# A float32 decoder trunk: two kinds of elementwise work moved from VectorE to adding transfers

## The chip, the cores and the metric

The kernel runs on one core of one Trainium2 chip. The metric is device microseconds of one execution. Three executions of the kernel before took 2245.96, 2246.11 and 2246.87 us; their median, 2246.11 us, is the time before.

## The reference

The program computes two layers of a decoder trunk in float32, over 528 tokens (16 learned meta tokens and 512 others) of 1024 features. Each layer has a feed-forward, a gated pair of mixers (a short convolution and an attention) and a second feed-forward, each with a layer norm behind it:

```python
def swiglu(x, w_up, w_down):
    gate, up = jnp.split(x @ w_up, 2, axis=-1)
    return (jax.nn.silu(gate) * up) @ w_down

for l in range(DEPTH):                       # DEPTH = 2, ALPHA = (2 * DEPTH) ** 0.25
    h = layer_norm(ALPHA * h + 0.5 * swiglu(h, ffn1_w_up[l], ffn1_w_down[l]), ln_g[l, 0], ln_b[l, 0])
    ...
    h = layer_norm(ALPHA * h + mix, ln_g[l, 1], ln_b[l, 1])
    h = layer_norm(ALPHA * h + 0.5 * swiglu(h, ffn2_w_up[l], ffn2_w_down[l]), ln_g[l, 2], ln_b[l, 2])
```

`w_up` is 1024 x 5632 (2816 gate and 2816 up features), `w_down` is 2816 x 1024. The change lies in the four feed-forwards only.

## The kernel before

Activations lie with their features on the partitions. A float32 product is run as three passes of float32r: each operand is split into hi (rounded to 12 significant bits) and lo (the exact rest), and hi\*hi, hi\*lo and lo\*hi are summed in PSUM (`mm3`, L90 to L93). A weight tile of 512 KB is loaded by SyncE into a float32 tile `raw` (`load`, L105), ScalarE casts it to `wh` (L111) and VectorE subtracts to get `wl` (L114); `operand` does both.

Four `raw` tiles (pool `rawp`) and four pairs of `wh`, `wl` (pool `wp`) serve the up products. The down weights use a pool of their own, `dp`, with two pairs and two raw tiles; two of the raw tiles of the up products come from that pool too, those for u2 and for the sum S1.

A feed-forward treats its 2816 features as 11 pairs of tiles. The first two pairs go through `up_start`; the other nine through `up_seven`, which makes gate and up of a pair by seven products of half the contraction (Winograd's form). It loads four tiles g1, u2, u1, g2 and forms four sums of them on VectorE: S1 = u1 + u2 (L431), S3 = g1 - u1 (L432, over u1), S2 = S1 - g1 (L433, over g1), S4 = g2 - S2 (L441, over g2). S1 is the operand of the sixth product in the order M1, M6, gate A, M7, up A, M5, M3. The other factors are splits of sums of the activations that Pool forms (L337) and ScalarE and VectorE split (L88).

The down products of a chunk of pairs run between the up products of the next chunk: `mid[0]` behind M6 and `mid[1]` behind M5, each with its weights split by `operand(weights(...), dp)` in `steps`. Their results are added to the residual `r` (L558 with the scaling in the first chunk, L564 later). In the first chunk the first feature tile also gives a shift for the norm: `shift_by` casts that tile to bfloat16 on VectorE (L253), one product spreads its mean (L254), ScalarE copies it (L256) and Pool subtracts it from `r` (L561). This happens once for each of the two token ranges. In the last feed-forward the down products have the tokens on the partitions and no shift.

A scheduler orders the instructions of each engine before the run, from the program's order and its own estimates of when each one is ready; on the chip each engine then runs its own list in that order. SyncE issues all weight loads; Pool issues a few small transfers and none in the feed-forwards but two near the end.

Of the kernel before, what the change touches and what calls it, by code (L numbers as in the profile page):

```python
# [14 lines left out]
AF = mybir.ActivationFunctionType  # L15
ALU = mybir.AluOpType
AX = mybir.AxisListType

P = 128
# [18 lines left out]
# token ranges (first, width): all tokens, and those behind the meta tokens  # L38
FULL = ((0, 256), (256, 272))
TRIM = ((16, 256), (272, 256))  # L40
# and in two equal parts
EVEN = {FULL: ((0, 264), (264, 264)), TRIM: TRIM}
# chunks of the feed-forward features, in pairs of tiles
# [8 lines left out]
def trunk(ctx: ExitStack, tc: tile.TileContext, x, meta, f1_up, f1_dn, w_in, b_gate, conv_w, qn_g, w_uq,  # L52
          kvn_g, w_ukv, w_bc, w_bm, w_o, f2_up, f2_dn, ln_g, ln_b, rope, out):
    """Float32 products run as three passes of float32r: an operand is hi + lo, hi its value rounded to 12
    significant bits and lo the exact rest, and hi*hi + hi*lo + lo*hi are summed in PSUM. Activations lie with
    their features on the partitions."""
# [8 lines left out]
    @contextmanager  # L65
    def scratch(n, t):
        """The eight banks of PSUM, n for psum() and the others for psum2(), and t tiles in SBUF."""
        with tc.tile_pool(name="psp", bufs=1, space=bass.MemoryType.PSUM, reuse_waits="tile") as pool, \
                tc.tile_pool(name="tmp", bufs=t, reuse_waits="tile") as tp:
            banks.append((pool, n))  # L70
            tps.append(tp)
            yield
            banks.pop()
            tps.pop()
# [23 lines left out]
    def unit(pool=wp, k=8, c=P):  # L98
        """A stationary operand, hi and lo, as [128, k, c]."""
        return [pool.tile([P, 1024], F32R, name=n)[:, :k * c].rearrange("p (k c) -> p k c", c=c)  # L100
                for n in ("wh", "wl")]
# [6 lines left out]
    def operand(raw, pool=wp, cut=1):  # L108
        """Split, in parts where others would wait for long."""
        u = unit(pool, raw.shape[1], raw.shape[2])  # L110
        S.copy(u[0], raw)  # L111
        n = raw.shape[1] // cut
        for k in range(0, raw.shape[1], n):
            V.tensor_tensor(u[1][:, k:k + n], raw[:, k:k + n], u[0][:, k:k + n].bitcast(F32), op=ALU.subtract)  # L114
        return u

    def columns(src, c, pool=wp):
        """128 columns of a matrix with 1024 rows."""
        return operand(load(src[:, c:c + P], KD, P), pool)

# [10 lines left out]
    # per-feature parameters as columns  # L131
# [11 lines left out]
    def tokens_in(xt, c0):  # L143
        """Two tiles of tokens, to the columns from c0."""
# [14 lines left out]
    with tc.tile_pool(name="xload", bufs=1, reuse_waits="tile") as xp, scratch(4, 1):  # L159
# [8 lines left out]
        # the array's clock falls while it waits for the first products' operands: of no use but for that  # L168
# [3 lines left out]
    def rest_in(pool):  # L172
        """The other tokens, and the parameters."""
# [21 lines left out]
    # Per-token statistics are taken with the tokens on the partitions, n of them in each of nt columns, and  # L195
    # spread back over the partitions of the features.
# [5 lines left out]
    def token_sums(ps, at, parts, n, nt):  # L202
        """Columns at, at + 2, ...: the means over D features of the parts together."""
# [6 lines left out]
    def spread(c, n, nt, act, ps):  # L210
        """c / D on all partitions."""
# [10 lines left out]
    def rsqrt(v, n, nt, by=float(D)):  # L222
        """by/sqrt(v): the exponent trick, a Newton step, and a step of third order."""
# [13 lines left out]
    class Norm:  # L237
        """Layer norm over the features of r, which holds twice the sum to norm. The sums of r and of its squares
        are taken as its last parts come; by then r has been moved by a value near the mean of each token, which
        keeps the variance exact."""  # L240
# [7 lines left out]
        def shift_by(self, q0, w, i):  # L248
            """The mean of the first features of each token, on all partitions: near the mean, so that a rounded
            one does."""  # L250
# [22 lines left out]
        def run(self, q0, w):  # L273
            """The rest, in steps between which the tensor engine should have something else to do."""
# [44 lines left out]
    def project_steps(ps, u, nk, rhs, q0, w, n=4):  # L319
        """The same, with a stop after each n of the products' parts."""  # L320
# [7 lines left out]
    def combos(hv, th, tl):  # L328
        """Sums and differences of the parts of x (halves of its features, 1 and 2, and of its tokens, A and B)
        that the seven products take, split, from r that holds x. By index: T1 = x1B - x1A,  # L330
        T2 = x2B - T1, T3 = x2B - x1B, -T4 = x2A - T2."""
# [8 lines left out]
    def up_start(hp, dp, w_up, hv, pending, th, tl, after, begin):  # L340
        """silu(gate) * up for the first two pairs of feature tiles. What the first tokens allow comes first."""
# [62 lines left out]
    def up_seven(hp, fp, w_up, f, hv, mid, th, tl):  # L404
        """silu(gate) * up for two feature tiles by seven products of halves (Winograd's form): rows are gate and
        up, the contraction is halved, columns are the two token ranges."""
# [20 lines left out]
        product(pa, operand(g1), x1a, True)              # M1  # L427
        for j in range(2):
            S.copy(m1[j], pa[j])
        s1 = raw_tile(fp).rearrange("p (k c) -> p k c", c=256)  # L430
        V.tensor_tensor(s1, u1, u2, op=ALU.add)          # S1  # L431
        V.tensor_tensor(u1, g1, u1, op=ALU.subtract)     # S3  # L432
        V.tensor_tensor(g1, s1, g1, op=ALU.subtract)     # S2  # L433
        product(pb, operand(g1), t2, True)               # M6
# [5 lines left out]
        product(pa, operand(g2), x2a, False)             # gate A  # L440
        V.tensor_tensor(g2, g2, g1, op=ALU.subtract)     # S4  # L441
        for j in range(2):
            S.activation(sg[j], pa[j], AF.Silu)
        product(pb, operand(u1), t3, False)              # M7
        for j in range(2):
            V.tensor_tensor(u3s[j], pb[j], m1[j], op=ALU.add)
        product(pb, operand(u2), nt4, False)             # up A but for M1
        for j in range(2):
            hh, hl = hs[j]
            V.tensor_tensor(m1[j], pb[j], m1[j], op=ALU.add)     # up A  # L450
            V.tensor_tensor(sg[j], sg[j], m1[j], op=ALU.mult)
            split(hh[:, qa:qa + w], hl[:, qa:qa + w], sg[j])
# [3 lines left out]
        product(pc, operand(s1), t1, True)               # M5  # L456
        if mid[2]:
            mid[3]()
        for j in range(2):
            V.tensor_tensor(u3s[j], pc[j], u3s[j], op=ALU.add)   # up B  # L460
        if not mid[2]:
            mid[1]()
        product(pc, operand(g2, wp, 2), x2b, False)             # M5 + M3
        if mid[2]:
            mid[3]()
        for j in range(2):
            hh, hl = hs[j]
            V.tensor_tensor(u2s[j], pc[j], u2s[j], op=ALU.add)   # gate B
# [5 lines left out]
    def ffn(l, w_up, w_dn, idx, hv, pending, tail=None):  # L474
        """r = 2 alpha x + swiglu(x), and its norm. The down products of a chunk run between the up products of the
        next. With tail, the last step: tokens go back to the partitions."""
        with tc.tile_pool(name="ffn_t", bufs=1, reuse_waits="tile") as ttp, \
# [17 lines left out]
            def steps(ci, hs, mps, parts=(0, 1)):  # L495
                def step(_=None):
                    for mp in mps:
                        u = by_tile(operand(weights(ci, mp, rawp), dp), len(hs))
# [84 lines left out]
    def down_tokens(l):  # L583
        """The last step's down products, with tokens on the partitions, and its norm."""
        rt = r.rearrange("p k t -> p (k t)")[:, 0:4 * D].rearrange("p (i d) -> p i d", d=D)

        def make(dp):
# [18 lines left out]
            def begin():  # L606
                """The residual, token tile by token tile, where the features' x was."""
# [28 lines left out]
            def end(tiles):  # L636
                """The norm of some tiles up to the scaling by the deviation, which is returned."""
# [36 lines left out]
    def gate(l, hv, wi, i, m2, dst, ps_of):  # L674
        """tanh of half the gates' arguments of two feature tiles: sigmoid(z) = (tanh(z / 2) + 1) / 2."""
# [7 lines left out]
    def attention(l, hv, wi, ap, yc, ym, pending):  # L683
# [39 lines left out]
        def filler():  # L723
            """The rest of the convolution's branch and the first gate, a few products at a time."""
# [46 lines left out]
        # strip[p, c]: masked where p > c - 128; strip2[p, c]: masked where c - 384 > p  # L771
# [9 lines left out]
        # keys and queries of a head: rows 0..63 plain, 64..95 rotary, 96 the maximum against -1  # L781
# [7 lines left out]
        with tc.tile_pool(name="low", bufs=1, reuse_waits="tile") as lp, \  # L789
# [6 lines left out]
            def first(part):  # L796
                """The projections, and the sums of squares of those that are normed."""
# [70 lines left out]
    def heads_in(l, hv, wi, ap, ckn, cqn, kt, zt, ym, filler, cosT, sinT,  # L868
                 strip, strip2):
        # keys and queries of 16 tokens, of two heads, whole: from row 97 on the unit matrix and the mask  # L870
# [11 lines left out]
        def group_weights(g):  # L882
            """Of four heads: keys and values and plain queries in one unit, rotary queries and their swap."""
# [17 lines left out]
        def values(ua):  # L901
            """Values by key tile, split, each with ones beside it; of the tokens that end a part whole as well."""
# [19 lines left out]
        def rotary(ub):  # L922
            """Rotary parts of the queries of four heads, 32 rows each."""
# [34 lines left out]
        def maxima(b):  # L958
            """The largest score of each query, into a column of zt."""
# [19 lines left out]
        def maxima_rows():  # L979
            """The maxima into row 96 of the queries."""  # L980
# [11 lines left out]
        def units(b, q0, w):  # L992
            """The key tiles of a head that 64 queries or more of a part see."""
            return [(b, k0) for k0 in KTILES[:4] if k0 < q0 + w - 64]

        def end_of(q0, w):
            """The last 16 queries of a part, where they see 16 keys of one tile more, their own: which."""
# [3 lines left out]
        def score(q0, w, b, k0):  # L1001
            """Exponentials of the masked scores of a key tile, split."""
# [14 lines left out]
        def score_end(s0):  # L1017
            """Exponentials of the scores of 16 tokens among themselves, of both heads."""
# [11 lines left out]
        def normal(pr, q0, w, a, b):  # L1030
            """Both heads of a pair: divide by the sums."""
# [16 lines left out]
        def weigh(job, vals, pr):  # L1048
            """Products with the values, and at the end of a part of the queries its division."""
# [124 lines left out]
def _rope_rows():  # L1174
    """Rotary factors by position, for four heads of 32 rows: the cosines and the signed sines."""
# [23 lines left out]
```

## Time and profile before

| | |
|---|---|
| median of the runs | 2246.11 us |
| span of the profiled execution | 2247.7 us |
| TensorE matmul busy | 2202.0 us (98%), 17989 instructions |
| VectorE busy | 1679.5 us (75%) |
| ScalarE busy | 974.5 us (43%) |
| Pool busy | 372.6 us (17%) |
| transfers | 202.80 MB, mean 90 GB/s; SyncE's queue 28.2% of 16 engines |

The profiled execution is one more execution than the three timed ones; of it the page gives the span, which is 1.6 us over the median. Busy time is the time in which an engine had an instruction of its own running; waits, semaphores and the issue of transfers do not count. Matmuls overlap each other, so a row's duration is longer than the distance to the next one. Names such as L114 are lines of the kernel before.

### The profile page before, as it was taken

Reading aid. Unit: us, or ns where it says so; the run is one execution under the profiler, and the core shown is the slowest. Engines: PE = TensorE matmul, PEld = TensorE weight load, DVE = VectorE, ACT = ScalarE, POOL = GpSimd, SP = SyncE. Lnnn points to the kernel's source line nnn. Section 1 sums busy time; section 2 is a strip of 40 time slices with the busy share of each in tenths; the row PEclk is TensorE's granted clock in tenths of the full one; section 3 lists DMA queues with packets and bytes.
Section 4 is the critical chain, followed back from the end, with each engine's and each line's share of the span. In section 5 each row is a group of like instructions: output and inputs, shape, how many; then the busy total and the mean of one; then the engine's idle time right before and its main releaser. Section 6 shows DMA issues by size and latency. Waiting matters only on the chain. (4 is left out here: it accounts for less than half of the span.)

```text
span 2247.7 us, 43950 instructions
## 1 busy us (share of the span) xinstructions
PE 2202.0 (98%) x17989; PEld 2181.9 (97%) x17989; DVE 1679.5 (75%) x3191; ACT 974.5 (43%) x1881; POOL 372.6 (17%) x487
## 2 busy tenths in 40 slices
PE   9999999999999999999999999999999999999998
PEld 8999999999999999999999999999999999999998
DVE  6777778876646777878778778787665568877887
ACT  4343344465533543434353433444655335443441
POOL 3210004211014512000242100042110155100000
PEclk9999999999999999999999999999999999999999
DMA  5232232222233223323323232322222332233322
GB/s 172 94 103 91 90 119 77 68 62 67 69 92 104 66 82 98 113 75 111 107 66 95 96 98 90 113 85 63 66 67 76 94 94 85 76 103 105 99 90 86
DMA packets 237418, 202.80 MB, mean 90 GB/s; under 512 B 6990, under 2 KB 233360, under 8 KB 237216
## 3 DMA queue, kind: packets, MB, share of 16 engines
q1 hardware_dynamic: 234880, 195.65, 28.2%
q0 software_dynamic: 2336, 4.34, 0.7%
q8 instruction: 141, 2.31, 0.4%
q14 instruction: 61, 0.50, 0.1%
HBM read 195.74 MB, written 2.10 MB: 88 GB/s over the span
## 5 line engine op out<-in xcount | busy, mean ns | idle before, releaser
L114 DVE TENSOR_TENSOR wl<-raw,wh 128x1024 fp32r<-128x1024 f32 (+1 forms) x490 | 560.5, 1145 | 250.0 <-ACT wh L111 248.5
L111 ACT CAST wh<-raw 128x1024 fp32r<-128x1024 f32 (+1 forms) x454 | 466.2, 1034 | 591.2 <-PE ps L92 174.3
L92 PE MATMUL ps<-xl,wh 128*128 128x256 f32 (+2 forms) x1760 | 501.7, 285 | 2.7 <-DVE xl L88 2.7
L91 PE MATMUL ps<-xh,wh 128*128 128x256 f32 (+2 forms) x1760 | 502.5, 286 | 0.1
L93 PE MATMUL ps<-xh,wl 128*128 128x256 f32 (+2 forms) x1760 | 501.6, 285 | 0.0
L92 PEld LDWEIGHTS ps<-xl,wh 128*128 128x128 f32 x1760 | 332.5, 189 | 4.3 <-DVE xl L88 4.0
L91 PEld LDWEIGHTS ps<-xh,wh 128*128 128x128 f32 x1760 | 333.0, 189 | 0.6 <-ACT xh L88 0.5
L93 PEld LDWEIGHTS ps<-xh,wl 128*128 128x128 f32 x1760 | 333.4, 189 | 0.0
L91 PE MATMUL ps<-th,wh 128*128 128x264 f32 (+1 forms) x1152 | 328.5, 285 | 0.0
L92 PE MATMUL ps<-tl,wh 128*128 128x264 f32 (+1 forms) x1152 | 327.6, 284 | 0.0
L93 PE MATMUL ps<-th,wl 128*128 128x264 f32 (+1 forms) x1152 | 326.9, 284 | 0.0
L91 PE MATMUL pf<-hh,wh 128*128 128x256 f32 (+1 forms) x864 | 246.7, 286 | 0.0
L93 PE MATMUL pf<-hh,wl 128*128 128x256 f32 (+1 forms) x864 | 246.3, 285 | 0.0
L92 PE MATMUL pf<-hl,wh 128*128 128x256 f32 (+1 forms) x864 | 245.3, 284 | 0.0
L92 PEld LDWEIGHTS ps<-tl,wh 128*128 128x128 f32 x1152 | 218.8, 190 | 0.0
L91 PEld LDWEIGHTS ps<-th,wh 128*128 128x128 f32 x1152 | 218.6, 190 | 0.1
L93 PEld LDWEIGHTS ps<-th,wl 128*128 128x128 f32 x1152 | 218.3, 189 | 0.0
L91 PE MATMUL pf<-xh,wh 128*128 128x256 f32 (+1 forms) x640 | 188.0, 294 | 0.0
L92 PE MATMUL pf<-xl,wh 128*128 128x256 f32 (+1 forms) x640 | 184.4, 288 | 0.0
L93 PE MATMUL pf<-xh,wl 128*128 128x256 f32 (+1 forms) x640 | 183.2, 286 | 0.0
L91 PEld LDWEIGHTS pf<-hh,wh 128*128 128x128 f32 x864 | 162.7, 188 | 0.0
L93 PEld LDWEIGHTS pf<-hh,wl 128*128 128x128 f32 x864 | 162.7, 188 | 0.0
(323 smaller groups left out, 4870.3 us busy)
## 6 DMA issues: line engine op xcount, KB each, us to landing
raw<-in_ffn_w_up_dram SPq DMA_DIRECT2D x176, 512.0 KB, 3.6
raw<-in_ffn_w_down_dram SPq DMA_DIRECT2D x80, 512.0 KB, 3.3
raw<-in_mix_w_in_dram SPq DMA_DIRECT2D x64, 512.0 KB, 3.7
raw<-in_w_o_dram SPq DMA_DIRECT2D x16, 512.0 KB, 3.9
raw<-in_ffn_w_down_dram SPq DMA_DIRECT2D x16, 256.0 KB, 2.6
raw<-in_w_br_conv_dram SPq DMA_DIRECT2D x8, 512.0 KB, 3.3
raw<-in_w_br_mla_dram SPq DMA_DIRECT2D x8, 512.0 KB, 3.3
out_dram<-r SPq DMA_DIRECT2D x8, 256.0 KB, 2.4
```

Source lines behind the costliest of these rows:

```text
L91: PE.matmul(ps, lhsT=lhs[0], rhs=rhs[0], start=first, stop=False, skip_group_check=more)
L92: PE.matmul(ps, lhsT=lhs[0], rhs=rhs[1], start=False, stop=False, skip_group_check=more)
L93: PE.matmul(ps, lhsT=lhs[1], rhs=rhs[0], start=False, stop=last, skip_group_check=more)
L111: S.copy(u[0], raw)
L114: V.tensor_tensor(u[1][:, k:k + n], raw[:, k:k + n], u[0][:, k:k + n].bitcast(F32), op=ALU.subtract)
```

## The change

Two edits, beside comments that are taken out. The down weights of all chunks but the last (80 operands) go through a new function: ScalarE writes -hi into `wl`, a transfer issued by Pool adds the raw tile to it, and ScalarE writes hi into `wh`. S1 is no longer a VectorE addition of u1 and u2: u1's part of the matrix is loaded a second time, into the tile of S1, and a transfer issued by Pool adds u2 to it. This happens 36 times.

```diff
+    def operand_dma(raw, pool=wp):
+        u = unit(pool, raw.shape[1], raw.shape[2])
+        S.activation(u[1], raw, AF.Copy, scale=-1.0)
+        G.dma_start(u[1], raw, accum_op=ALU.add)
+        S.copy(u[0], raw)
+        return u
...
-        s1 = raw_tile(fp).rearrange("p (k c) -> p k c", c=256)
-        V.tensor_tensor(s1, u1, u2, op=ALU.add)          # S1
-        V.tensor_tensor(u1, g1, u1, op=ALU.subtract)     # S3
+        s1 = load(w_up[0:512, D_FF + f * P:D_FF + f * P + 256], KH, 256, fp)
+        G.dma_start(s1, u2, accum_op=ALU.add)
+        V.tensor_tensor(u1, g1, u1, op=ALU.subtract)
...
-                        u = by_tile(operand(weights(ci, mp, rawp), dp), len(hs))
+                        u = by_tile(operand_dma(weights(ci, mp, rawp), dp), len(hs))
```

## Rows read from the trace of the kernel before

**Rows 1.** Busy time by engine in one steady pair (instructions), clock, DMA share, GB/s.
```profile
128.60:160.70 32.10, 32.10 (x267) 32.10 (x266) 25.87 (x41) 12.43 (x20) 3.54 (x3) 1.00 0.32 99
```

**Rows 2.** What TensorE waited for: us in total, times, longest us.
```profile
PE pf L219 <- DVE t L218: 11.1, 13, 1.9
PE ps L254 <- DVE t L253: 7.3, 3, 2.7
...
PE ps L92 <- DVE xl L88: 2.7, 6, 0.7
```

**Rows 3.** VectorE in order of time around the first such wait: start, duration, line.
```profile
72.53 0.29 DVE L253 CAST t<-r 128x256 bf16<-128x256 f32 x1
75.67 1.23 DVE L431 TENSOR_TENSOR raw<-raw 128x1024 f32<-128x1024 f32 x1 [2.84 <-DMA raw<-in_ffn_w_up_dram]
...
77.14 1.22 DVE L432 TENSOR_TENSOR raw<-raw 128x1024 f32<-128x1024 f32 x1
78.28 0.78 DVE L558 SCALAR_TENSOR_TENSOR r<-r,pf 128x272 f32<-128x272 f32 x2
78.97 0.82 DVE L253 CAST t<-r 128x272 bf16<-128x272 f32 x1
```

**Rows 4.** The stretches behind the three waits: columns as in rows 1.
```profile
80.00:82.00 2.00, 2.00 (x10) 2.00 (x10) 0.00 (x0) 1.39 (x3) 1.25 (x2) 0.50 0.00 0
830.00:832.00 2.00, 2.00 (x12) 2.00 (x12) 0.20 (x1) 1.66 (x3) 1.37 (x2) 0.54 0.00 0
1205.00:1207.00 2.00, 2.00 (x14) 2.00 (x14) 0.62 (x1) 1.62 (x3) 1.50 (x2) 0.66 0.01 4
```

**Rows 5.** VectorE groups by shape: count, busy us, mean ns, idle before.
```profile
L114 DVE TENSOR_TENSOR wl<-raw,wh 128x1024 fp32r<-128x1024 f32 x402 | 499.5, 1244 | 196.8 <-ACT wh L111 196.1
L114 DVE TENSOR_TENSOR wl<-raw,wh 128x512 fp32r<-128x512 f32 x88 | 61.0, 693 | 53.2 <-ACT wh L111 52.4
...
L431 DVE TENSOR_TENSOR raw<-raw 128x1024 f32<-128x1024 f32 x36 | 45.5, 1264 | 39.2 <-DMA raw<-in_ffn_w_up_dram 37.4 <-issue 1.5 <-DVE r L599 0.3
```

**Rows 6.** SyncE's issues of the four up loads ahead of rows 3.
```profile
62.59 0.37 SPq L105 DMA_DIRECT2D raw<-in_ffn_w_up_dram  x1
67.76 1.89 SPq L105 DMA_DIRECT2D raw<-in_ffn_w_up_dram  x2
70.38 0.37 SPq L105 DMA_DIRECT2D raw<-in_ffn_w_up_dram  x1
```

**Rows 7.** Transfers by line: count, KB each, median us from issue to landing.
```profile
raw<-in_ffn_w_up_dram SPq DMA_DIRECT2D x176, 512.0 KB, 3.6
...
qt<-qrl POOLq DMA_DIRECT2D x8, 64.0 KB, 2.3
...
wl<-in_ln_b_dram POOLq DMA_DIRECT2D x1, 512.0 KB, 5.2
```

**Rows 8.** ScalarE in order of time: a steady pair's cast of down weights.
```profile
152.15 1.05 ACT L111 CAST wh<-raw 128x1024 fp32r<-128x1024 f32 x1 [2.08 <-DMA raw<-in_ffn_w_down_dram]
```

**Rows 9.** TensorE in order of time: first down product, first of M3.
```profile
169.33 0.28 PE L91 MATMUL pf<-hh,wh 128*128 128x256 f32 x1
...
192.71 0.28 PE L91 MATMUL ps<-xh,wh 128*128 128x264 f32 x1
```

**Rows 10.** VectorE in order of time, in the same steady pair.
```profile
170.55 1.22 DVE L114 TENSOR_TENSOR wl<-raw,wh 128x1024 fp32r<-128x1024 f32 x1 [0.52 <-ACT wh L111]
...
183.72 1.22 DVE L433 TENSOR_TENSOR raw<-raw 128x1024 f32<-128x1024 f32 x1
...
187.40 0.77 DVE L460 TENSOR_TENSOR t<-ps,t 128x264 f32<-128x264 f32 x2
```

**Rows 11.** VectorE in order of time, in the first pair of the first feed-forward.
```profile
45.98 1.22 DVE L433 TENSOR_TENSOR raw<-raw 128x1024 f32<-128x1024 f32 x1
...
48.39 1.23 DVE L114 TENSOR_TENSOR wl<-raw,wh 128x1024 fp32r<-128x1024 f32 x1 [0.84 <-ACT wh L111]
50.54 1.23 DVE L114 TENSOR_TENSOR wl<-raw,wh 128x1024 fp32r<-128x1024 f32 x1 [0.92 <-ACT wh L111]
```

## The prediction

> **What bounds the kernel now.** I looked first at the busy time in one steady stretch, then at what TensorE waited for, then at the costliest VectorE groups, and last at the order of time around each TensorE wait. One pair of feature tiles in the feed-forward takes 32.10 us, and TensorE is busy for all of it with 267 matmuls, 0.120 us each [rows 1]. VectorE is busy 25.87 us of it, ScalarE 12.43, Pool 3.54, the DMA engines 0.32. So work taken off VectorE inside a steady pair buys nothing by itself: what can be won is only the time in which TensorE stands. The waits of TensorE name it [rows 2]: 11.1 us in the norms, 7.3 us in three waits for the cast at L253, 2.7 us for parts of x. Only the last two stand beside an instruction that the change removes.
>
> **The three waits.** They fall once in each of the first three feed-forwards, where the first down products give the shift of the norm. In order of time VectorE casts the first shift operand at 72.53, then sits idle 2.84 us until a load of up weights has landed, does S1 (L431) at 75.67, then three residual updates (L558) with S3 (L432, 77.14) between them, and the second cast at 78.97 [rows 3]. TensorE needs that second cast and stands. The granted clock says that the stop costs more than its length: behind the three waits it is 0.50, 0.54 and 0.66 over two microseconds, so the lower level of 1.2 GHz for most of the stretch, after TensorE had idled over 2 us; in these stretches it did 10, 12 and 14 matmuls [rows 4] where 2.00 / 0.120 = 16.7 fit. That is (6.7 + 4.7 + 2.7) x 0.120 = 1.7 us more. The three places hold 7.3 + 1.7 = 9.0 us.
>
> **The change part by part.**
> *S1 leaves VectorE.* 36 additions go, 45.5 us in all, with 39.2 us of idle time before them [rows 5]. Which load did S1 wait for? It reads u1 and u2. u1, g1 and g2 share the four raw tiles, u2 takes the pool of the down weights. The four loads go out at 62.59, 67.76, 69.28 (the row's 67.76 + 1.89 - 0.37) and 70.38 [rows 6]; a load lands after 3.6 us [rows 7]. I read the last one as u2's, which has to wait for its own pool: landing near 74, and near 75.6 with three loads in flight. S3 = g1 - u1 does not need u2. It takes S1's place behind the first cast with u1 landed at the latest by 69.28 + 3.6 = 72.9. Then S3 runs 72.9 to 74.1 (1.22), the three updates take 1.2 as now (0.78 for two), and the second cast is done at about 75.7 instead of 79.8. TensorE's wait of 2.7 us ended with that cast (78.97 + 0.82 = 79.8), so it began at 77.1: the wait goes with 1.4 us to spare, and with it the slow stretch: -9.0 us over three places. What is late next there: nothing that I find; the operands of the following products stand ready well ahead (17 us for the one looked at below).
>
> *The lo parts of the down weights leave VectorE.* 80 operands (64 of 1024 columns, 16 of 512) times 1244 and 693 ns [rows 5] are 79.6 + 11.1 = 90.7 us. All lie beside TensorE work, so 0 us, and the loss of it is no gain. ScalarE takes a second pass of 1.05 us in its place [rows 8], 64 x 1.05 + 16 x about half of it = 76 us, raising its 12.43 us of 32.10 by 2.1: room enough, 0 us.
>
> *The adding transfer.* The trace shows none. As the lower bound I take the 64 KB transfer between tiles on Pool's queue, 2.3 us; as the upper one twice the slower 512 KB transfer on that queue, 2 x 5.2 = 10.4 us, since it reads both operands [rows 7]. I take 5.2, the row nearest in size and queue.
> The Trainium skill's page "Collectives: The Full Stack" (The bandwidth ceiling: the fold count and why AG ≠ RS ≠ AR) says that an add in the DMA path runs at half the copy rate because it needs two source reads; by that the transfer lies near the upper end, and the sum would be the 2240 to 2241 worked out below for it. No run here shows an add.
> For the down weights: the hi of the next pair's first unit is cast at 152.15 [rows 8] and its product starts at 169.33 [rows 9], 17.2 us later. Two ScalarE passes and 10.4 us from issue to landing need 12.5. So lo is in time even at the upper end: 0 us. The raw tile is held longer, by the transfer less the old subtraction, 5.2 - 1.2 = 4 us (9 at the upper end). The load at 62.59 goes into such a tile; it moves to about 66.6, still ahead of the one at 67.76, and at the upper end it passes that one by 4 us, which the 1.4 us to spare do not cover: u1 would land at 71.8 + 3.6 = 75.4, the second cast end at 78.1, and 1 us of each wait stay, 2240 to 2241 in all.
> For S1: its load takes the slot that is free after the subtraction at 170.55 [rows 10], so 171.8 + 3.6 = 175.4, and the adding transfer lands at 180.6. S2 (L433), which now waits for it, stands at 183.72 because it overwrites g1, so it has 3.1 us of margin at 5.2 us and is 2.1 us late at 10.4. Queued behind S2 on VectorE are the evacuations, first of all L460 at 187.40, which TensorE needs before M3 at 192.71 [rows 9, 10]: 5 us more. So a steady pair loses nothing up to some 13 us: 0 us.
> In the first pair of a feed-forward S2 stands at 45.98 and VectorE has gaps of only 0.84 and 0.92 us ahead of the passes at 48.39 and 50.54 [rows 11]; both loads are possible long before, as their pool is empty there, so 0 us, with a price below.
>
> *Traffic and Pool.* A pair moves six tiles of 512 KB now at a DMA share of 0.32; one load and three transfers more make 10/6 of it, 0.53, or 0.69 if an add counts twice. Not full: 0 us. Pool issues 116 transfers more, three or four to a pair in which it is busy 3.54 us. In the first down chunk the transfers share its queue with the residual updates that wait for the shift; those write r, which no product of that chunk reads, so a delay there costs 0 us.
>
> *Sum.* The span is 2247.7 us, 1.6 above the median of 2246.11 that I forecast from; the difference is carried over as it is. 2246.1 - 9.0 = **2237.1 us**.
>
> **The rivals.**
> *No gain (2246).* S1's place in the order was chosen by the scheduler from its own estimates; with S1 gone it may put something else there, a lo pass or S3 behind later loads (the retained raw tiles speak for it), and the second cast comes as late as now. For it: the 1.4 us to spare are few. Against it: the named wait is for one particular load. A part of the gain would read 2241 to 2246.
> *Slower at the first pairs (2253).* If the load or the transfer of S1 is put behind other work in its queue at the start of a feed-forward, S2 waits, and the splits of the token combinations, queued behind it, come late for the second product. It decides where the lateness exceeds the two gaps, 0.84 + 0.92 = 1.8 us. At the upper end of the transfer, 5.2 us later than taken, it is 5.2 - 1.8 = 3.4 us at each of four places, and a slow stretch of 0.6 us each: +16, less 9 if the other gain still comes, 2253.
> *Slower in every pair (2300).* The same transfer above 13 us, because it also changes the number format. At 15 us each of the 32 steady pairs loses 2 us: 2237 + 64 = 2301. For it: nothing here shows an add or a change of format. Against it: the 512 KB transfers of [rows 7] land in 3.6 and 5.2 us.
> *The transfer doesn't give lo* (it may round raw before the add): that would spoil digits but cost the same time.
>
> **How the numbers follow.** Chances: forecast 0.50, no gain 0.27, slower at first pairs 0.14, slower everywhere 0.09. The forecast's own range is 2233 (the 2.7 us at parts of x go as well, where S1 also stands in line, and a slow stretch behind them) to 2242. The range 2233 to 2254 leaves out the case in every pair and the worse half of the one at the first pairs. A difference of 0.2%, 4.5 us, is what a measurement can tell: below 2241.6 lies most of the forecast, 0.47; between, the no-gain case with its edges, 0.32; above 2250.6 the rest, 0.21.
>
> **What would show it.** Right: no wait for the cast at L253 in TensorE's list and a granted clock near 1.00 where it was 0.50; L432 close behind the first cast with no long wait for a load; VectorE's busy time lower by about 136 us and ScalarE's higher by 76, with TensorE's busy time unchanged. The transfers should land in about 5 us, and L433 should wait for them in no steady pair. Wrong: L253 still named, with another line in S1's place; new TensorE waits at the second product of the first pair; or L433 idle on a transfer in pair after pair.

## The result, and the profile after

The changed kernel takes 2319.12 us (median of four, 2314.39 to 2323.78), the kernel before 2246.49 in the same comparison: 1.0324 times as long, 95% interval 1.0308 to 1.0341. That is 72.6 us slower, where 9 us faster was forecast, and beyond every case that was priced, the worst of which was 2301. Lines of the kernel after are those of before plus 8 from L117 of before on: S1's transfer is L439, S3 L440, S2 L441, S4 L449, the evacuation behind M7 (VectorE's reading of that product out of PSUM) L454; -hi of a down weight is L120, its transfer L121, a token sum L345.

The head of the page of the kernel after:

```profile
span 2315.2 us, 44380 instructions
...
PE 2214.6 (96%) x17989; PEld 2190.3 (95%) x17989; DVE 1567.3 (68%) x3075; ACT 1041.0 (45%) x1961; POOL 456.9 (20%) x603
```

TensorE does the same 17989 matmuls, and Pool's 603 instructions are the 487 of before and the 116 issues. Of the 67.5 us by which the span grew, its busy time holds 12.6 (2214.6 - 2202.0) and its idle time 54.9 (100.6 - 45.7). VectorE has 112 us less to do, and the kernel is slower: the time is in waits.

What TensorE waits for after (columns as in [rows 2]):

```profile
PE ps L91 <- DVE t L454: 40.5, 13, 8.6
PE ps L91 <- DVE t L379: 14.4, 3, 4.8
PE pf L625 <- DVE t L623: 7.6, 1, 7.6
```

The norms' row is about that of before (10.3 us for 11.1). The three waits for the cast are gone. L454 and L379 are new, and the one at L625 was 3.4. With two smaller new rows, 5.6 together, that is 40.5 + 14.4 + 4.2 + 5.6 = 64.7 us more; the casts' 7.3 and the 2.7 at xl of [rows 2] went: 54.7, close to the 54.9 us of added idle time. A steady pair of after, and two stretches behind new waits (columns as in [rows 1]):

```profile
128.60:160.70 32.10, 32.10 (x264) 31.90 (x263) 21.35 (x37) 14.49 (x23) 7.41 (x7) 1.00 0.66 165
68.00:70.00 2.00, 2.00 (x11) 2.00 (x10) 1.54 (x3) 1.92 (x3) 0.00 (x0) 0.50 1.03 205
231.00:233.00 2.00, 1.84 (x8) 1.84 (x9) 2.00 (x4) 0.00 (x0) 0.00 (x0) 0.50 0.04 8
```

A steady pair is as full as in [rows 1], with VectorE 4.5 us less busy. Behind a wait the granted clock is 0.50, the level of 1.2 GHz, and 11 or 8 matmuls stand where 18 or 19 stand at 1.00 (before, 84 to 90 us): the busy time that grew. VectorE of after around the first shift, in order of time:

```profile
77.24 1.22 DVE L440 TENSOR_TENSOR raw<-raw 128x1024 f32<-128x1024 f32 x1 [2.30 <-DMA raw<-in_ffn_w_up_dram]
...
80.30 0.29 DVE L261 CAST t<-r 128x256 bf16<-128x256 f32 x1
...
81.31 0.30 DVE L261 CAST t<-r 128x272 bf16<-128x272 f32 x1
```

Transfers of after by line (count, KB each, median us to landing):

```profile
raw<-in_ffn_w_up_dram SPq DMA_DIRECT2D x212, 512.0 KB, 4.4
...
wl<-raw POOLq DMA_DIRECT2D x64, 512.0 KB, 4.8
...
raw<-raw POOLq DMA_DIRECT2D x36, 512.0 KB, 4.8
...
wl<-raw POOLq DMA_DIRECT2D x16, 256.0 KB, 3.2
```

Both casts now stand behind S3, 1.0 us apart, where [rows 3] had S1 and S3 between them. The wait is gone, as forecast, but here not by the forecast's way: S3 stands ahead of the first cast and has waited for a load, the second cast ends at 81.6 and not at 75.7, and TensorE, late itself by then, takes it at 84.3. The forecast's times show in e2 below. The price of a transfer came true, 4.8 us for the 5.2 taken.

**Place A: the start of a feed-forward.** Pool in order of time (start, duration, line, and in brackets the idle time before with what ended it), after:

```profile
38.35 0.93 POOL L439 DMA_DIRECT2D raw<-raw  x1 [33.04 <-PE ps L93]
38.96 1.10 POOL L345 TENSOR_TENSOR t<-r 128x264 f32<-128x264 f32 x1
51.05 0.89 POOL L121 DMA_DIRECT2D wl<-raw  x1 [10.99 <-ACT t L373]
51.67 1.06 POOL L345 TENSOR_TENSOR t<-r,t 128x264 f32<-128x264 f32 x1
...
63.83 0.93 POOL L345 TENSOR_TENSOR t<-r,t 128x264 f32<-128x264 f32 x1
```

The same of before:

```profile
22.58 0.76 POOL L337 TENSOR_TENSOR t<-r 128x264 f32<-128x264 f32 x1 [17.31 <-DVE r L191]
31.29 0.75 POOL L337 TENSOR_TENSOR t<-r,t 128x264 f32<-128x264 f32 x1 [7.95 <-DVE r L191]
...
56.77 0.95 POOL L337 TENSOR_TENSOR t<-r,t 128x264 f32<-128x264 f32 x1
```

After, the first sum stands behind S1's transfer and the second behind a down weight's transfer, which waits for ScalarE's -hi. ScalarE of after, -hi:

```profile
49.70 1.05 ACT L120 ACTIVATE wl<-raw 128x1024 fp32r<-128x1024 f32 x1
```

All sums but the first, spread from 31 to 58 before, are done from 51.67 to 64.8. Their splits on VectorE end at 66.4, and behind them in its list stands L379 (the product of gate and up), for which TensorE waits until 66.81, the first of the two rows below. This comes three times, 4.8 us each; in the last feed-forward the wait of 7.6 us at L625 takes its place.

**Place B: a chunk of one pair.** TensorE of after at the two places, in order of time:

```profile
66.81 0.59 PE L91 MATMUL ps<-xh,wh 128*128 128x264 f32 x1 [4.82 <-DVE t L379]
...
231.16 0.59 PE L91 MATMUL ps<-th,wh 128*128 128x264 f32 x1 [5.91 <-DVE t L454]
```

SyncE's loads ahead of the second place:

```profile
211.34 0.37 SPq L105 DMA_DIRECT2D raw<-in_ffn_w_up_dram  x1
224.36 0.37 SPq L105 DMA_DIRECT2D raw<-in_ffn_w_up_dram  x1
```

VectorE there:

```profile
228.94 1.22 DVE L440 TENSOR_TENSOR raw<-raw 128x1024 f32<-128x1024 f32 x1 [9.02 <-DMA raw<-in_ffn_w_up_dram]
...
230.68 0.43 DVE L454 TENSOR_TENSOR t<-ps,t 128x264 f32<-128x264 f32 x1
```

VectorE has nothing to do for 9.02 us, because S3 of the *next* pair is next in its list and its load was issued at 224.36, after SyncE had waited for a raw tile. Behind it, with one lo part between, stands the evacuation of *this* pair's M7, which needs nothing that comes late but TensorE's result, and TensorE cannot go on without it. This comes in the chunk of one pair of all four feed-forwards: these four of the 13 waits at L454, 5.2 to 8.6 us, make 25.4 of the 40.5. The next longest, 4.6 us at 1520.59, ends a feed-forward's last pair, where no S3 follows; its evacuation stands behind splits of the last down weights.

The kernel before has S3 ahead of the evacuations too:

```profile
215.89 1.22 DVE L432 TENSOR_TENSOR raw<-raw 128x1024 f32<-128x1024 f32 x1
...
217.89 0.42 DVE L446 TENSOR_TENSOR t<-ps,t 128x264 f32<-128x264 f32 x1
```

There the load had landed, and the order cost nothing. At the place above a tile is held for longer than a transfer's own time: on Pool the down weight's transfer of 217.94 stood behind S1's of 217.39, ahead of which Pool had idled 11.4 us. SyncE's waits for a held raw tile over the run of the kernel after (us in total, times, longest):

```profile
SPq L105 <- DMA wl<-raw: 578.9, 78, 17.1
```

VectorE's, at S3 and S2:

```profile
DVE raw L440 <- DMA raw<-in_ffn_w_up_dram: 94.0, 30, 11.6
...
DVE raw L441 <- DMA raw<-raw: 57.6, 17, 5.3
```

### The profile page after: what moved, and what is told of

Its sections match the earlier page's. It is cut to its first block, busy times and chain, and to the rows that moved or that the text cites. A ratio compares the mean times of both kernels' runs of the same rounds, so it can differ in the third digit from the quotient of the medians.

```text
span 2315.2 us, 44380 instructions
## 1 busy us (share of the span) xinstructions
PE 2214.6 (96%) x17989; PEld 2190.3 (95%) x17989; DVE 1567.3 (68%) x3075; ACT 1041.0 (45%) x1961; POOL 456.9 (20%) x603
## 3 DMA queue, kind: packets, MB, share of 16 engines
q1 hardware_dynamic: 253888, 214.53, 30.5%
q0 software_dynamic: 19040, 60.97, 13.6%
## 4 chain that ended last, share of the span: by engine, by line
PE 62%; DVE 9%; DMA 8%; issue 2%; ACT 2%; POOL 0%; DVEq 0%; POOLq 0%; ACTq 0%; SPq 0%
PE ps L91 13%; PE ps L92 13%; PE ps L93 13%; PE pf L91 6%; PE pf L92 6%; PE pf L93 6%; DMA raw<-in_ffn_w_up_dram 3%; DMA raw<-raw 2%; DVE wl L114 2%; DVE tl L88 2%; DMA wl<-raw 2%; DMA raw<-in_ffn_w_down_dram 1%; ACT wh L111 1%; PE ps L978 1%; PE ps L1014 1%
## 5 line engine op out<-in xcount | busy, mean ns | idle before, releaser
L114 DVE TENSOR_TENSOR wl<-raw,wh 128x1024 fp32r<-128x1024 f32 (+1 forms) x410 | 476.4, 1163 | 242.6 <-ACT wh L111 241.1
L111 ACT CAST wh<-raw 128x1024 fp32r<-128x1024 f32 x374 | 390.4, 1047 | 363.6 <-PE ps L92 163.3
L91 PE MATMUL ps<-xh,wh 128*128 128x256 f32 (+2 forms) x1760 | 506.2, 288 | 19.0 <-DVE t L379 14.4
L91 PE MATMUL ps<-th,wh 128*128 128x264 f32 (+1 forms) x1152 | 333.3, 289 | 41.8 <-DVE t L454 40.5
L121 POOL DMA_DIRECT2D wl<-raw x80 | 70.5, 881 | 575.0 <-ACT wl L120 362.4
```

The costliest lines, as they stand in the source:

```text
L91: PE.matmul(ps, lhsT=lhs[0], rhs=rhs[0], start=first, stop=False, skip_group_check=more)
L121: G.dma_start(u[1], raw, accum_op=ALU.add)
```

## The experiments

Times are medians beside the kernel before in the same comparison; ratios are to it. Edits of e8, e9, e10 and e14 are against the kernel before, all others against the kernel after. Lines shift by a few from run to run; where an experiment's text names L379, L454 or L625, their counterparts are meant.

**e1: the down weights' transfers alone**, S1 as before.

```diff
-        s1 = load(w_up[0:512, D_FF + f * P:D_FF + f * P + 256], KH, 256, fp)
-        G.dma_start(s1, u2, accum_op=ALU.add)
+        s1 = raw_tile(fp).rearrange("p (k c) -> p k c", c=256)
+        V.tensor_tensor(s1, u1, u2, op=ALU.add)
```

> The change's first part alone: lo of the down weights by -hi and an adding transfer; S1 stays an addition on VectorE. Theory: the loss has two causes, (a) at the start of each feed-forward the transfer for the first down weight stands in Pool's queue ahead of the sums of the activations and holds them until ScalarE has written -hi, some 22 us of TensorE waits plus a slow clock behind them over four places; (b) the transfers hold the raw tiles longer, so SyncE issues the up loads later and VectorE's sums, late, hold the evacuations behind them (line 446 of the kernel before). Both belong to this part, so most of the loss stays: 2290 to 2305 us, and the three waits for the cast at L253 stay too or are longer, as S1 still stands ahead of it. Rival, the extra load and transfer of S1 are the cause of (b): then only (a) is left, about 2272 us.

2280.95 us, 1.0157 [1.0142, 1.0172], between the two. Place A is whole (14.5 us at L379, 7.6 at L625), L454 has 20.2. So the down weights make place A by themselves and half of place B. Against the expectation the casts' waits fell to 1.0 us, with S1 still on VectorE between the casts (80.48, the second cast at 83.79): TensorE, late from place A, came there no sooner. So in the kernel after their going is no proof of S1's.

**e2: S1's transfer alone.**

```diff
-  u = by_tile(operand_dma(weights(ci, mp, rawp), dp), len(hs))
+  u = by_tile(operand(weights(ci, mp, rawp), dp), len(hs))
```

> The change's second part alone: S1 by a second load and an adding transfer; the down weights are split as before. Theory: the transfer of S1 stands ahead of the activation sums on Pool too, but ends its wait at 38 us, so the start loses nothing; raw tiles are free as early as before; the three waits for the cast at L253 go, 9 us less: 2236 to 2242 us. Rival, S1's transfer is what comes late in every pair (S2 waits 57.6 us for it in the changed kernel): 2270 to 2290 us.

2255.37 us, 1.0043 [1.0028, 1.0058]: both missed. The casts' waits are gone, at the first place with the second cast done at 75.9 (forecast 75.7) and TensorE there at 77.2 (77.1). But L454 has 9.3 us in 7 waits, three of them, 6.7 us, where the casts' waits had been, and a later evacuation, L468, has 5.3 us in 5. Pool of e2 around the first, in order of time:

```profile
78.33 0.89 POOL L439 DMA_DIRECT2D raw<-raw  x1 [20.42 <-DMA raw<-in_ffn_w_up_dram]
78.95 1.74 POOL L569 TENSOR_TENSOR r<-r,rs 128x256 f32<-128x256 f32 x2
80.34 1.77 POOL L569 TENSOR_TENSOR r<-r,rq 128x272 f32<-128x272 f32 x2
```

VectorE of e2 there:

```profile
75.58 0.30 DVE L261 CAST t<-r 128x272 bf16<-128x272 f32 x1
...
78.98 3.69 DVE L114 TENSOR_TENSOR wl<-raw,wh 128x512 fp32r<-128x512 f32 x1 [2.75 <-ACT wh L111]
```

TensorE of e2:

```profile
83.07 0.39 PE L91 MATMUL ps<-th,wh 128*128 128x264 f32 x1 [2.23 <-DVE t L454]
```

Pool's residual updates wait behind S1's transfer, which waits for its load. They then run just when VectorE makes a lo part, and that takes 3.69 us instead of the 0.69 of [rows 5]; the evacuation behind it, at 82.59, is late. It is the same at the other two places (3.45 and 3.92 us): the wait was moved, by Pool's queue.

**e3: -hi by ScalarE, the addition by VectorE**, no transfer, S1 as before.

```diff
         S.activation(u[1], raw, AF.Copy, scale=-1.0)
-        G.dma_start(u[1], raw, accum_op=ALU.add)
+        V.tensor_tensor(u[1], raw, u[1].bitcast(F32), op=ALU.add)
         S.copy(u[0], raw)
```

> The down weights' lo from ScalarE's -hi, but VectorE adds the raw tile, no transfer; S1 on VectorE as before. It has the second ScalarE pass of the change and no other part of it. Theory: the pass costs nothing, 2244 to 2250 us. Rival, ScalarE's second pass delays its queue: 2260 us or more.

2246.29 us, 1.0000 [0.9991, 1.0010]. ScalarE's second pass (67.6 us more busy time; 76 were forecast) cost nothing, as forecast; the change's loss comes with the transfers and S1's second load.

**e4: place A as before**, the rest changed (S1 of the first pair and the first chunk's down weights on VectorE).

```diff
+        if f == 4:
+            s1 = raw_tile(fp).rearrange("p (k c) -> p k c", c=256)
+            V.tensor_tensor(s1, u1, u2, op=ALU.add)
...
+  u = by_tile((operand if ci == 0 else operand_dma)(weights(ci, mp, rawp), dp), len(hs))
```

> The changed kernel with the first pair's S1 and the first chunk's down weights of each feed-forward as before; all else by transfers. Theory: the waits of the first pairs go (line 371 of the kernel before, three of 4.8 us, and the one of 7.6 us in the last feed-forward) with the slow clock behind them, 22 + 4 us less than the changed kernel: about 2292 us; the waits for late sums stay. Rival, the late start is only another form of the retained raw tiles or of loaded DMA engines: the waits stay, 2310 us or more.

2302.39 us, 1.0249 [1.0232, 1.0266], between the two. The waits at L379 are gone and that at L625 is 3.4 us; the evacuation keeps 42.3 us. Place A is worth 16.7 us here.

**e5: Pool's order mended**, transfers kept: the down weights' transfers behind the last token sum, S1's (but for the first pair) behind the down transfer that precedes it in the program.

```diff
+        with tc.issue_after(pool_last["combo"].ins):
+            pool_last["wl"] = G.dma_start(u[1], raw, accum_op=ALU.add)
...
+            with tc.issue_after(pool_last["wl"].ins):
+                G.dma_start(s1, u2, accum_op=ALU.add)
```

> The changed kernel with Pool's order tied: the transfers of down weights stand behind the last sum of the activations (L345 of the changed kernel), and each S1 transfer but a feed-forward's first stands behind the down-weight transfers that precede it in the program. The same work, the same tiles. Theory: the start waits go (22 us and some 4 of slow clock), and the four long waits at the chunk of one pair (5.9, 5.2, 5.7, 8.6 us at L454) shrink to about 1 us each, since there an S1 transfer that waits for its load stood ahead of a transfer that would free a raw tile: 25 us and slow clock less again, about 2266 us; the short waits at L454 stay, as raw tiles are still held. Rival: the long waits come from the retention alone, and only the start goes: about 2293 us.

2275.81 us, 1.0138 [1.0122, 1.0154]: 43.3 us back, 10 us less than the theory had. Place A is gone, the evacuation still has 22.6 us.

**e6: a raw tile of its own for every second down weight**, at the price of three scratch tiles. **e7: e5 and e6.**

```diff
-FFN_SCR, MIX_SCR = (4, 14), (6, 8)
+FFN_SCR, MIX_SCR = (4, 11), (6, 8)
...
+  tc.tile_pool(name="ffn_x", bufs=1, reuse_waits="tile") as xp, \
...
+  u = by_tile(operand_dma(weights(ci, mp, xp if mp % 2 else rawp), dp), len(hs))
```

> The changed kernel with one raw tile more: every second down weight is loaded into a tile of its own, outside the four shared ones (three of the 14 scratch tiles are given up for the room). Theory: SyncE's up loads no longer wait for transfers of these, and most of the 40 us of waits at L454 go; the start waits stay: 2275 to 2295 us. Rival, the transfers load the DMA engines or Pool's order alone counts, and the tile changes nothing: 2310 us or more.

> Pool's order tied as in e5_pool_order and the raw tile of e6_raw_more, together. Theory: if order and retention are the whole loss, what remains is within 10 us of the kernel before, 2237 to 2256 us. Rival, a third cause (the doubled traffic, S2's wait for its transfer): 2265 us or more.

e6: 2266.41 us, 1.0093 [1.0079, 1.0108], 52.7 us back, 9 us below the theory's range. TensorE's waits in e6:

```profile
PE ps L91 <- DVE t L379: 13.7, 3, 4.7
...
PE ps L91 <- DVE t L454: 4.1, 5, 1.1
```

Place B is nearly gone, place A stays. In the chunk of one pair S3 now stands at 204.14 and the evacuation at 220.31: its load comes early enough. e7: 2262.33 us, 1.0067 [1.0052, 1.0082], between theory and rival; the two cures do not add up, 16 us remained, and the evacuation behind M7 has 8.1 us again.

**e9: the scratch alone. e10: three raw tiles in place of four, no transfers. e11: e1 with e6's tile.**

> The kernel before with 11 scratch tiles in the feed-forward in place of 14, the price at which e6 and e7 bought their raw tile. Theory (what e7 still loses to before, 16 us, comes from the transfers and their order): the three scratch tiles are worth nothing, 2244 to 2249 us. Rival (e7's remainder is the scratch that it gave up): 2254 us or more, with TensorE waits at the evacuations in the pairs, and then e6 and e7 understate what the raw tile gives back.

> The kernel before with three raw tiles for the up products in place of four; no transfer is added. It tests the step that held a raw tile for nothing. Theory (the up loads wait for a tile, and a tile held longer makes S3 and what is queued behind it on VectorE late): slower by 10 to 45 us, 2256 to 2290, with SyncE's loads and VectorE's S3 and S4 waiting longer and TensorE at the evacuation behind S3. Rival (four tiles are more than enough, the lateness came from Pool's order alone): 2243 to 2250 us.

> e1 (the down weights' transfers alone, S1 on VectorE; 2281 us) with a raw tile of its own for every second down weight, as in e6. Theory (two prices, Pool's order at the start and held tiles): TensorE's 20.2 us at L454's counterpart fall below 6, the waits at the token sums (14.5 us at L379, 7.6 at the norm) stay: 2258 to 2270 us. Rival (in e1 the lateness is Pool's order alone): 2276 us or more. Rival (held tiles are all of it): below 2252.

e9: 2249.34 us, 1.0013 [1.0004, 1.0023]; the scratch costs 2.8 us and doesn't explain e7. e11: 2256.53 us, 1.0037 [1.0024, 1.0049], 24.4 us back, a little more than the two-price theory had, with L454 down to 1.1 and place A left (13.2 and 8.0). e10 went against my theory: 2249.49 us, 1.0012 [1.0002, 1.0023]. Its casts' waits are gone, and 5.5 us at the evacuation and 5.9 at a down weight's hi stand in their place, so a tile less costs some 11 us of waits, a fraction of place B (3 us net; 16 against e8 below, where the casts' waits are gone as well). VectorE of e10 in the chunk of one pair:

```profile
216.56 0.43 DVE L446 TENSOR_TENSOR t<-ps,t 128x264 f32<-128x264 f32 x1
...
217.70 1.23 DVE L431 TENSOR_TENSOR raw<-raw 128x1024 f32<-128x1024 f32 x1
218.84 0.43 DVE L446 TENSOR_TENSOR t<-ps,t 128x264 f32<-128x264 f32 x1
...
220.66 1.22 DVE L432 TENSOR_TENSOR raw<-raw 128x1024 f32<-128x1024 f32 x1
```

Here the scheduler put S3 (L432) *behind* both evacuations (L446), where the kernel before has it ahead. So not the number of tiles alone, but S3's place in the list was the suspect.

**e12: e5, and S3 of a pair (a feed-forward's first excepted) behind the evacuations of the pair before. e13: this edge alone.** Tiles and transfers stay.

```diff
+        with tc.issue_after(evac["u3"].ins) if f > 4 else nullcontext():
+            V.tensor_tensor(u1, g1, u1, op=ALU.subtract)
...
+            evac["u3"] = V.tensor_tensor(u3s[j], pb[j], m1[j], op=ALU.add)
```

> e5 (Pool's order mended; 2275.8 us, TensorE 22.6 us at the evacuations L460) with one more ordering edge: from the second seven-product pair on, S3 of a pair stands on VectorE behind the two M7 evacuations of the pair before. Tiles, transfers and loads stay. Theory (S3 of the next pair, waiting for a late load, stands ahead of this pair's evacuations): the waits at L460's counterpart fall below 6 us and with them the slow stretches, 2242 to 2256 us. Rival (a late load is late whatever stands behind it; S3's own product M7 or S2 waits in its place): 2266 us or more, with TensorE waits at the splits of S3 or S2.

> The changed kernel (2319 us) with the edge of e12 alone, Pool's order as it was. Theory (two separate faults, Pool's order at the start and S3 ahead of the evacuations): the 40.5 us at L454 fall below 12, the waits at the start (14.4 at the token sums, 7.6 at the norm) stay: 2268 to 2284 us. Rival (Pool's queue makes the S1 transfer late too, so S2 holds the evacuations in S3's place): 2300 us or more, with VectorE waiting at S2 for the transfer.

e12: 2240.50 us, 0.9970 [0.9958, 0.9981], faster than before. e13: 2264.13 us, 1.0070 [1.0054, 1.0087], with 6.0 us at the evacuation and place A whole (14.5 and 7.6). Both are as the theory had it, and a little better (e12 by 1.5 us, e13 by 4). e13 shows the mechanism by itself. In the chunk of one pair the load that S3 needs is still late (issued at 219.95, the one before it at 207.15; after: 224.36 and 211.34). SyncE and VectorE of e13 there (L456 is the evacuation, L442 S3):

```profile
219.95 0.37 SPq L106 DMA_DIRECT2D raw<-in_ffn_w_up_dram  x1
```

```profile
222.45 0.43 DVE L456 TENSOR_TENSOR t<-ps,t 128x264 f32<-128x264 f32 x1 [0.31 <-PE ps L94]
...
225.85 1.23 DVE L442 TENSOR_TENSOR raw<-raw 128x1024 f32<-128x1024 f32 x1 [2.97 <-DMA raw<-in_ffn_w_up_dram]
```

S3 waits 2.97 us, and 2.65, 2.93 and 4.48 in the other three such chunks, and TensorE waits at none of these four places. Of the 6.0 us left at the evacuation, 5.5 stand in last pairs, where no S3 follows. TensorE's waits in e12 (L462 is the evacuation, L448 S3):

```profile
PE ps L93 <- DVE t L462: 3.8, 5, 1.9
PE pf L633 <- DVE t L631: 3.4, 1, 3.4
```

SyncE's in e12:

```profile
SPq L107 <- DMA wl<-raw: 548.4, 78, 20.8
```

VectorE's at S3 in e12:

```profile
DVE raw L448 <- DMA raw<-in_ffn_w_up_dram: 1.9, 1, 1.9
```

SyncE waits for the held tiles as long as in the kernel after, 548 us to 579, and it costs TensorE next to nothing: S3 waits 1.9 us where it waited 94.0. VectorE of e12 in the chunk of one pair:

```profile
213.34 0.42 DVE L462 TENSOR_TENSOR t<-ps,t 128x264 f32<-128x264 f32 x1
...
214.67 0.43 DVE L462 TENSOR_TENSOR t<-ps,t 128x264 f32<-128x264 f32 x1 [0.31 <-PE ps L95]
215.01 1.22 DVE L448 TENSOR_TENSOR raw<-raw 128x1024 f32<-128x1024 f32 x1
```

The evacuations come before S3, as in e10, and S3's load has landed. (An edge lets the scheduler plan the other queues anew too, so not every microsecond is S3's own.)

**e8: the kernel before, S1 of the second seven-product pair behind the second shift cast, in the first three feed-forwards. e14: the kernel before, S1 and S3 of every pair but a feed-forward's first behind the evacuations of the pair before.** No transfers.

```diff
+            self.cast = V.tensor_copy(b, r[:, 0, q0:q0 + w])
...
+        if f == 6 and cast:
+            with tc.issue_after(cast().ins):
+                V.tensor_tensor(s1, u1, u2, op=ALU.add)
```

```diff
+        with tc.issue_after(evac["u3"].ins) if f > 4 else nullcontext():
+            V.tensor_tensor(s1, u1, u2, op=ALU.add)          # S1
+            V.tensor_tensor(u1, g1, u1, op=ALU.subtract)     # S3
```

> The kernel before, with one edge in VectorE's order: the S1 that waits for its load in the second pair of the first three feed-forwards stands behind the second cast of the shift instead of ahead of it. No transfer. Theory of the prediction for the three waits: 7.3 us of wait and 1.7 of slow clock go, 2236 to 2239 us. Rival: the wait moves to the next evacuation behind S1, and nothing is gained: 2244 us or more.

> The kernel before, without any transfer, with S1 and S3 of a pair behind the two M7 evacuations of the pair before, the edge that took e12 to 2240.5 us. Theory (in e12 the order brings the gain and the transfers nothing): the three waits for the cast at L253 go as in e8, 2231 to 2238 us, so e12's transfers cost some 4 to 9 us. Rival (with S1 still on VectorE, S1 and S3 behind the evacuations are too late for M6 and M7): 2246 us or more. Rival (VectorE's relief is worth something once the order is right): 2240 to 2246 us, level with e12 or above.

e8: 2233.56 us, 0.9945 [0.9933, 0.9958], 12.6 us faster than before. e14: 2232.76 us, 0.9939 [0.9925, 0.9952], 13.4 us faster. In both the casts' waits are gone and nothing took their place. So the forecast's gain was there to have, by order alone, and e12 with all its transfers is 7.7 us behind e14. Both e8 and e14 beat the kernel before and the one after.

## Why the prediction was wrong

*The three waits go, and with them 9.0 us.* The waits went, in e2 at the forecast's times, in the kernel after with place A's lateness in front of them. The 9.0 us were there, and more: e8 and e14 took 12.6 and 13.4. The term that was too small is the slow clock. The prediction read it over two microseconds behind each wait; in the next two of the kernel before (columns as in [rows 1]) it goes on:

```profile
82.00:84.00 2.00, 2.00 (x16) 2.00 (x15) 1.35 (x3) 0.33 (x2) 0.25 (x1) 0.84 0.00 0
832.00:834.00 2.00, 2.00 (x12) 2.00 (x12) 1.12 (x3) 0.06 (x1) 0.12 (x1) 0.60 0.00 0
1207.00:1209.00 2.00, 2.00 (x11) 2.00 (x11) 1.44 (x3) 0.00 (x0) 0.00 (x0) 0.50 0.00 0
```

With the clocks of [rows 4], 2 us times what each lacks to 1.00 makes 4.7 us in all, an estimate, for the 1.7 of the prediction; with the waits' 7.3 that is 12.0. (The prediction set its 10, 12 and 14 against 16.7 from the mean distance; they count every matmul that touches the stretch, and so counted 18 or 19 stand in 2 us at 1.00.) The sentence that failed is "What is late next there: nothing that I find": in e2 the evacuation behind M7 was late in the same places.

*The lo parts leave VectorE: 0 us; ScalarE's second pass: 0 us.* Right for the pass (e3). No run takes the lo parts off VectorE without a transfer; that it gains nothing fits e12, which has 115 us less VectorE work than e14 and is slower. VectorE's busy time fell by 112 us, not 136. The groups of the lo parts fell by 84.1 of the 90.7 us, S1's 45.5 went, and the splits of the sums took longer: the main group of them 45.2 us for 26.9 with the same 48.

*The adding transfer: 5.2 us.* Right in the median, 4.8. The half-rate rule of the Trainium skill's page "Collectives: The Full Stack" (The bandwidth ceiling: the fold count and why AG ≠ RS ≠ AR) was read as a landing time at the upper end; it does not show there, and the page has it of two ring collectives. In the load on the transfer engines there is more of it: the steady pair's DMA share went from 0.32 to 0.66, between the 0.53 and the 0.69 that the prediction gave for an add that counts once and twice. By the page of the kernel after, the queue of the adds took 13.6% of the engines' time for 60.97 MB, SyncE's, of loads from device memory, 30.5% for 214.53 MB: 1.6 times as much a megabyte.

*"Not full: 0 us."* True of the steady pair (0.66), not of every stretch: from 68 to 70 us the share is 1.03, and a load's median landing went from 3.6 to 4.4 us. No run tests this by itself; e12 has the whole traffic of the kernel after (278 MB) and is 7.7 us behind e14, so there the traffic's price is no more than of that size.

*Pool: "a delay there costs 0 us".* This is the first step that failed. The prediction named only the residual updates as sharing Pool's queue. The token sums run on Pool too and were left out; the second rival had their splits late, but by way of S2 on VectorE. A transfer that must wait for ScalarE or for a load stops all of Pool's arithmetic behind it. The residual updates were not free either: in e2, late behind S1's transfer, they made VectorE's lo part, and by it the evacuation, late. Its worth: 16.7 us (after to e4) or 23.6 (e13 to e12), and 43.3 (after to e5) where e5 mends place B in part as well; the rival gave 16.

*"The raw tile is held longer ... still ahead of the one at 67.76."* This is the second. The price of the hold was read at one place, in which the loads had time. In the chunk of one pair they had not, and there the hold met S3, which the list had ahead of work that was ready. Worth: 35.3 us (e5 to e12) to 55.0 (after to e13). Both edges together give 78.6 us (after to e12); each alone takes 19.7 us of it that the other would take too. The first rival named it ("S3 behind later loads"), but priced it as a gain lost, not as a loss.

*"A steady pair loses nothing up to some 13 us", and S2 waits "in no steady pair".* The first is right for the stretch shown, with TensorE full. The second is wrong: S2 waited 57.6 us in 17 of its 36 places, none of them a first pair. And L468, to whose counterpart L460 the prediction gave 5 us of margin, made TensorE wait 4.3 us in 7 places (one of the two smaller new rows above).

*What stays open.* With both faults mended e12 stands 3.4 us above the forecast, inside its own range of 2233 to 2242, but with two order edges that the change did not have, so this is no success of the forecast. Against e14 its transfers still cost 7.7 us; where these sit, but for the 3.8 us at the evacuations, was not pursued, nor was e7's remainder.

## What to carry to other kernels

Before handing an engine's work to a transfer, read the whole list of the engine that issues it: each issue with a wait stops the arithmetic behind it, and the tile that it reads is held until it lands. Then look, in the tightest chunk and not in the steady one, for an instruction that waits for a late load ahead of one that TensorE needs; putting the first behind the second was worth 55 us here (after to e13), and 112 us less VectorE work nothing that shows. Try the order alone first: one edge in the old kernel gave all the gain that the change was to bring.

## What the runs showed of the hardware

VectorE's subtraction of 512 columns took 3.69 us beside Pool's four updates in e2, from 78.98 to 82.67, for 0.69 us at other times; Pool's four ran from 78.95 to 82.11. The Trainium skill's page "SBUF — State Buffer" (Who interferes with whom) says that a VectorE instruction with two inputs in SBUF contends with a Pool instruction that reads SBUF, and calls the contention an exclusive lock. The trace agrees that VectorE waited; it waited 3.0 us, for about all four of Pool's instructions and not for one of some 0.8, and at the two like places it took 3.45 and 3.92 us. An add by transfer lands in 4.8 us for 512 KB and 3.2 us for 256 KB, and its issue keeps Pool for 0.9 us.
